# A transformer layer on one core: loads and waits of x's last tokens, of the attention's first pair, and of five modulation steps put elsewhere in the order

## The chip, the cores and the metric

The kernel runs on one core of a Trainium2 chip. The metric is the device time of one execution in microseconds (us), lower is better; several runs are made, and their median is compared. A core has five engines, each with its own instruction queue worked off in order: TensorE (PE in the profile; its weight loads are PEld), VectorE (DVE), ScalarE (ACT), GpSimd (POOL) and SyncE (SP, which here issues most of the DMAs). Engines wait for one another on semaphores.

## The reference, cut to what matters

One layer over 512 latent tokens x and 256 context tokens ctx, width 1024, in float32: a SwiGLU half-step, two mixers side by side (a neighbourhood attention and a gated delta rule) merged by gates, and a second SwiGLU half-step. Shift, scale and gate of each sublayer are columns of silu(c) @ w_ada.

```python
def ffn_sublayer(h, m, i, w_up, w_down):
    shift, scale, gate = sub_mod(m, i)
    y = swiglu(modulate(h, shift, scale), w_up, w_down)
    return post_ln(DEEPNORM_ALPHA * h + 0.5 * gate * y, ln_g[i], ln_b[i])
x = ffn_sublayer(x, mod_x, 0, ffn1_w_in, ffn1_w_out)
ctx = ffn_sublayer(ctx, mod_c, 0, ffn1_w_in, ffn1_w_out)
qa, ka, va, qkv_b, z_b, a_b, b_b, ga, gb = split_proj(modulate(x, shift_x, scale_x) @ w_in)
...
o_a = na_latent(grid(qa), grid(ka), grid(va), kc_h, vc_h, na_rpb)
o_b = gdn_output(o_lat2[0] + jnp.flip(o_lat2[1], axis=2), z_b, gdn_norm_w)   # o * norm * silu(z)
y = sigmoid(ga) * (o_a @ w_pa) + sigmoid(gb) * (o_b @ w_pb)
x = post_ln(DEEPNORM_ALPHA * x + gate_x * (y @ w_o), ln_g[1], ln_b[1])
x = ffn_sublayer(x, mod_x, 2, ffn2_w_in, ffn2_w_out)
```

## The kernel before

Matmuls are made in three passes: each float32 operand is split into a rounded high part (a cast on ACT) and the rest (a subtraction on DVE), and high x high, high x low and low x high are summed in PSUM. So nearly every tile exists as a pair: weights are loaded raw (wr, ra), cast to wh on ACT (`split`, L137) and subtracted to wl on DVE (L139); modulated tokens become uxh and uxl in the same way, and the mixer's output obh and obl.

A scheduler orders the instructions of each engine from their data and from its own timeline; `tc.issue_after(x)` holds the instructions inside it behind instruction x. Tiles come from pools with a fixed number of buffers, so a load waits until the tile's last reader is done. `Stream` loads and splits the weights some steps ahead; `behind` names, for an item, the instructions behind which its cast and its subtraction are put. `marks` holds instructions that such waits name.

Three places matter.

*The third section's steps.* The first half-step runs its units over x, then eight units over the context tokens (N1 = 8, f from 0; 48 matmuls each). Between units `ada_step` runs a step of `ada_gen`: it loads 128 rows of w_adaT (512 KB), and DVE multiplies them with silu(c) for x and for ctx and sums them up (two instructions of L280, tile adap). With the last row tile of a section one instruction (L303) adds the bias to colx, one to colc. Behind the units, TensorE transposes these columns to rows (`to_row`, L242), and the down projection follows (L211).

*The last tokens of x.* Behind the first half-step's down projection of x, `finish1` normalises each of the four blocks of 128 tokens (y), and `to_u` transposes y on TensorE, scales and shifts it on ACT into u (four pieces of 128 columns to a half, L151), and splits each half into uxh and uxl. These run beside the context's down projection. Its end frees PSUM tiles through `evac1` (DVE: h, L635, then x1c, L636), and then come the projections into the mixers: `fill_spill` multiplies uxh and uxl with w_in's columns for z, 24 matmuls to a group; in the order the first three groups are ps_5263, ps_5298 and ps_5333, with the weights wh_5174, wh_5180 and wh_5259. `finish1(fc, "c", ...)` normalises the context tokens (squares on ACT, L644; DVE, L649 and L651; y at L660), beside these.

*The attention's first pair.* `attend` works on a pair of heads m and four blocks b of 128 queries: scores on TensorE (sc, L1446), bias and maximum on DVE (L1448, L1450), exponentials on ACT (pr, L1454), transposes of pr on TensorE and their copies on ACT (pT, L1463), values transposed on TensorE (from vst) and copied by DVE (vw, L1430), and the product po (L1472). `att_load` loads qa, ka, kc, bias and va of the next pair and splits them. The lines ahead of the pairs load the delta rule's output ob and its gate z from DRAM, multiply them on DVE (L1491) and split the product; `gated` multiplies it with w_pb in slots between the blocks.

## Time and profile before

| | us |
|---|---|
| three runs | 1501.2, 1498.06, 1495.04 |
| median | 1498.06 |
| the profiled execution's own time | 1493.83 |
| its span (first to last instruction) | 1492.1 |
| TensorE busy | 1436.7 (96%) |
| VectorE busy | 1146.2 (77%) |
| ScalarE busy | 662.5 (44%) |
| GpSimd busy | 214.5 (14%) |
| 248.56 MB moved | mean 167 GB/s |

The mean granted clock of TensorE over the span was 0.99 of full speed. A row of a timeline gives the start, the length, engine, line, operation, output<-input with shapes, the count, and in brackets how long the engine had been idle ahead of it and what ended that.

### The profile page before, as it was taken

To read this page: it belongs to the slowest core of one execution; us is meant where nothing else is said; L and a number is where in the kernel's file an instruction comes from. 1 tells how busy PE (TensorE), PEld (TensorE's weight loads), DVE (VectorE), ACT (ScalarE), POOL (GpSimd) and SP (SyncE) were. 2 spreads that over 40 slices of the span, in tenths; PEclk is the share of its full clock that TensorE was granted. 3 is DMA by queue.
4 is the path that set the end of the run, shared out by engine and by line. 5 is a ranking of instruction groups with operands and counts; after the bars stand their busy time and mean duration, and the time that the engine had idled before them with its cause. 6 is when DMAs were issued, how large, how long until landed. Compare 5 with 4: busy or idle time off the path is not lost.

```text
span 1492.1 us, 23919 instructions
## 1 busy us (share of the span) xinstructions
PE 1436.7 (96%) x9117; PEld 1259.7 (84%) x9117; DVE 1146.2 (77%) x1975; ACT 662.5 (44%) x1090; POOL 214.5 (14%) x262
## 2 busy tenths in 40 slices
PE   6999999999999999999999899989999999999997
PEld 4789889999998777989887778867788999998886
DVE  8686969999987565768787896667668799886627
ACT  5435513434333286546544434367526454444310
POOL 1000000000000121323301002242321022220001
PEclk9999999999999999999999999999999999999999
DMA  9675764444569443222477523374244133233732
GB/s 371 208 257 212 254 239 174 151 171 156 170 210 401 178 174 121 93 92 81 152 231 205 171 68 125 105 254 140 99 170 156 57 132 109 88 111 136 261 98 84
DMA packets 109236, 248.56 MB, mean 167 GB/s; under 512 B 29049, under 2 KB 44481, under 8 KB 109121
## 3 DMA queue, kind: packets, MB, share of 16 engines
q1 hardware_dynamic: 104480, 229.40, 45.3%
q0 software_dynamic: 3056, 12.33, 2.2%
q10 hardware_dynamic: 1586, 5.32, 0.9%
q8 instruction: 71, 1.16, 0.3%
q14 instruction: 43, 0.35, 0.1%
HBM read 215.50 MB, written 31.50 MB: 166 GB/s over the span
## 4 chain that ended last, share of the span: by engine, by line
PE 72%; DVE 11%; DMA 9%; issue 3%; ACT 3%; POOL 2%; SPq 1%; DVEq 0%; ACTq 0%; POOLq 0%
PE ps L211 15%; PE pm L192 5%; PE pm L193 5%; PE pm L194 5%; PE ps L535 4%; PE ps L534 4%; PE ps L533 4%; PE ps L193 4%; PE ps L194 4%; PE ps L192 4%; PE ps L1692 3%; PE ps L1694 3%; PE ps L1693 3%; PE pc L1049 2%; DVE wl L139 2%
## 5 line engine op out<-in xcount | busy, mean ns | idle before, releaser
L139 DVE TENSOR_TENSOR wl<-wr,wh 128x1024 fp32r<-128x1024 f32 (+1 forms) x184 | 225.9, 1232 | 117.6 <-ACT wh L137 117.2
L137 ACT CAST wh<-wr 128x1024 fp32r<-128x1024 f32 (+1 forms) x184 | 185.3, 1013 | 265.1 <-PE pm L193 63.9
L192 PE MATMUL pm<-uxh,wh 128*128 128x512 f32 x320 | 131.7, 412 | 0.0
L194 PE MATMUL pm<-uxh,wl 128*128 128x512 f32 x320 | 126.5, 395 | 1.6 <-DVE wl L139 1.6
L193 PE MATMUL pm<-uxl,wh 128*128 128x512 f32 x320 | 126.2, 395 | 0.0
L211 PE MATMUL ps<-wh,hx 128*128 128x512 f32 x352 | 95.9, 391 | 0.7 <-ACT wh L137 0.7
L211 PEld LDWEIGHTS ps<-wh,hx 128*128 128x128 f32 x352 | 65.9, 188 | 15.1 <-ACT wh L137 1.1
L280 DVE SCALAR_TENSOR_TENSOR adap<-wr,crow 128x1024 f32<-128x1024 f32 x61 | 74.3, 1218 | 0.7 <-ACT crow L288 0.3
L194 PEld LDWEIGHTS pm<-uxh,wl 128*128 128x128 f32 x320 | 60.8, 190 | 14.8 <-DVE wl L139 1.8
L192 PEld LDWEIGHTS pm<-uxh,wh 128*128 128x128 f32 x320 | 60.9, 190 | 11.0 <-ACT spill L796 0.2
L193 PEld LDWEIGHTS pm<-uxl,wh 128*128 128x128 f32 x320 | 61.0, 191 | 10.4
L192 PE MATMUL ps<-uh,wh 128*128 128x256 f32 (+1 forms) x208 | 68.5, 329 | 0.8 <-ACT wh L137 0.8
L193 PE MATMUL ps<-ul,wh 128*128 128x256 f32 (+1 forms) x208 | 67.7, 325 | 0.0
L194 PE MATMUL ps<-uh,wl 128*128 128x256 f32 (+1 forms) x208 | 67.6, 326 | 0.0
L114 POOL TENSOR_TENSOR rs<-ve,mhalf 128x1 f32<-128x1 f32 (+2 forms) x46 | 47.3, 1030 | 139.8 <-DVE ve L110 137.4
L193 PE MATMUL ps<-uxl,wh 128*128 128x256 f32 (+1 forms) x192 | 61.3, 321 | 1.6 <-DVE uxl L139 1.6
L192 PE MATMUL ps<-uxh,wh 128*128 128x256 f32 (+1 forms) x192 | 60.6, 323 | 1.6 <-ACT uxh L137 1.4
L194 PE MATMUL ps<-uxh,wl 128*128 128x256 f32 (+1 forms) x192 | 60.9, 320 | 0.0
L137 ACT CAST wh<-ra 128x1024 fp32r<-128x1024 f32 x31 | 32.6, 1052 | 60.3 <-PE ps L534 20.2
L533 PE MATMUL ps<-ur,wh 128*128 128x384 f32 x168 | 56.5, 336 | 0.0
L534 PE MATMUL ps<-ur,wh 128*128 128x384 f32 x168 | 56.4, 336 | 0.0
L533 PE MATMUL ps<-uh,wh 128*128 128x384 f32 x168 | 56.4, 336 | 0.0
(502 smaller groups left out, 4257.6 us busy)
## 6 DMA issues: line engine op xcount, KB each, us to landing
wr<-in_w_adaT_dram SPq DMA_DIRECT2D x64, 512.0 KB, 4.7
wr<-in_up_dram SPq DMA_DIRECT2D x56, 512.0 KB, 3.5
wr<-in_win_dram SPq DMA_DIRECT2D x52, 512.0 KB, 3.3
wr<-in_dn_dram SPq DMA_DIRECT2D x51, 512.0 KB, 3.5
...
```

The costliest lines, as they stand in the source:

```text
L114: G.tensor_tensor(rs[:], ve[:], mhalf[:, 0:n], ALU.pow)
L137: S.copy(hi, src)
L139: marks["lo"] = V.tensor_tensor(lo, src, hi.bitcast(F32), ALU.subtract).ins
L192: T.matmul(ps, a, uh[:, k, :], start=(k == 0), stop=False)
L193: T.matmul(ps, a, ul[:, k, :], start=False, stop=False)
L194: marks["mm"] = T.matmul(ps, b, uh[:, k, :], start=False, stop=(k == nk - 1)).ins
L211: T.matmul(banks[t][d][:, c0:c1], a[:, sl], b[:, d * 512 + c0:d * 512 + c1], start=first and j == 0, stop=last and j == 2)
L280: V.scalar_tensor_tensor(pr[:], raw[:], 1.0, crow, op0=ALU.mult, op1=ALU.mult, accum_out=col[:, c:c + 1])
L533: T.matmul(ps[:], a, mh, start=k == 0, stop=False)
L534: T.matmul(ps[:], a, ml, start=False, stop=False)
L535: T.matmul(ps[:], b, mh, start=False, stop=k == 3)
L1692: T.matmul(ps[:], a, uh[:, k], start=k == 0, stop=False)
```

## The change

The third section's five extra steps stand in other context units; x's last token block is scaled and split half by half, with the work that stood beside it put behind; and the loads and products of ob and z go into the attention's first pair, in tiles of yb, with the next pair's casts put behind named copies.

```diff
@@ -134,11 +134,11 @@
     def split(src, hi, lo, behind=()):
 
         with tc.issue_after(behind[0]) if behind and behind[0] else nullcontext():
-            S.copy(hi, src)
+            marks["hi"] = S.copy(hi, src).ins
         with tc.issue_after(behind[1]) if behind else nullcontext():
             marks["lo"] = V.tensor_tensor(lo, src, hi.bitcast(F32), ALU.subtract).ins
 
-    def to_u(tp, pp, xn, uh, ul, c0, scale, shift, tag="u32", behind=()):
+    def to_u(tp, pp, xn, uh, ul, c0, scale, shift, tag="u32", behind=(), halves=False):
 
         u32 = tl(tp, [P, KT, P], tag)
         for hb in range(2):
@@ -146,9 +146,10 @@
             for q in range(4):
                 k = hb * 4 + q
                 T.transpose(ps[:, q, :], xn[:, k * P:(k + 1) * P], ident)
-            for q in range(4):
-                k = hb * 4 + q
-                S.activation(u32[:, k, :], ps[:, q, :], AF.Identity, bias=shift[:, k:k + 1], scale=scale[:, k:k + 1])
+            with tc.issue_after(marks["hi"]) if halves and hb else nullcontext():
+                for q in range(4):
+                    k = hb * 4 + q
+                    S.activation(u32[:, k, :], ps[:, q, :], AF.Identity, bias=shift[:, k:k + 1], scale=scale[:, k:k + 1])
             ks = slice(hb * 4, hb * 4 + 4)
             split(u32[:, ks], uh[:, ks, c0:c0 + P], ul[:, ks, c0:c0 + P], behind)
         return u32
@@ -476,7 +477,7 @@
     for f in range(N1):
         hc.append(h_c())
         ffn_unit(tp, pp, ws.get(), ws.get(), uch, ucl, NCT, *hc[-1])
-        ada_step(f in (2, 3, 4, 5, 6))
+        ada_step(f in (0, 1, 3, 4, 5))
     rows_out(tp, "fs", 2)
     accd = tl(dp, [6, P, D], "accd")
     sild = tl(dp, [1, D], "sild")
@@ -665,7 +666,9 @@
 
     def u2(p, pp, kind, t, y):
         uh, ul, col = (uxh, uxl, colx) if kind == "x" else (uch, ucl, colc)
-        to_u(p, pp, y, uh, ul, t * P, secs(col, 4), secs(col, 3))
+        to_u(p, pp, y, uh, ul, t * P, secs(col, 4), secs(col, 3), halves=kind == "x" and t == 3)
+        if kind == "x":
+            ux_done[:] = marks["hi"], marks["lo"]
 
     wp2, close_wp2 = pool("w1b")
     NT = 4
@@ -730,9 +733,10 @@
 
     def after(t, j, banks):
         if j == NT - 1:
-            nms.append(evac1(lp, banks, x1c[t], x1c[t], gc))
-
-    FIN1 = (0, 2, 5, 8)
+            with tc.issue_after(ux_done[1]) if t else nullcontext():
+                nms.append(evac1(lp, banks, x1c[t], x1c[t], gc))
+
+    FIN1, ux_done = (0, 2, 5, 8), []
     down(pp, ws, hc, 2, 0, tail[:-NT], between, after, post=tail[-NT:], n=N2)
     order = [("z", m) for m in range(4)]
     for h in range(4):
@@ -743,6 +747,7 @@
     order += [(n, m) for n in ("pb", "pa") for m in range(8)]
     src = [I["wab"] if n == "ab" else I["w" + n][m] if n in ("pa", "pb") else I["win"][WIN_IDX[(n, m)]] for n, m in order]
     ws2 = Stream(wp, [(w, "a") if j < 24 and j % 3 == 2 else w for j, w in enumerate(src)], WB, 2)
+    ws2.behind = {1: tuple(ux_done), 2: tuple(ux_done)}
     ws2.fill(2)
     close_wp2()
     close_lp()
@@ -1004,7 +1009,8 @@
         for _ in fill_spill(ga_, "z", m, zd):
             pass
         if m > 1:
-            ys.append(finish1(fc, "c", len(ys), x1c[len(ys)], nms[4 + len(ys)]))
+            with tc.issue_after(ux_done[0]), tc.issue_after(ux_done[1]):
+                ys.append(finish1(fc, "c", len(ys), x1c[len(ys)], nms[4 + len(ys)]))
     units = []
     for h in range(4):
         units += [decay()] * (h == 2) + [unit_q(h), unit_k(h), unit_v(h), unit_kc(h), unit_vc(h)]
@@ -1365,13 +1371,14 @@
     close_gb()
     ne, close_ne = pool("ne", "right")
 
-    def att_load(p, m):
+    def att_load(p, m, behind=(None, None)):
 
         qk = []
         for n, c, src in (("qa", NX, qad), ("ka", NX, kad), ("kc", NCT, kcd)):
             hi, lo = tl(p, [P, c], n + "h", 1, F32R), tl(p, [P, c], n, 1, F32R)
             nc.sync.dma_start(lo[:].bitcast(F32), src[m])
-            S.copy(hi[:], lo[:].bitcast(F32))
+            with tc.issue_after(behind[0]) if behind[0] else nullcontext():
+                S.copy(hi[:], lo[:].bitcast(F32))
             G.tensor_tensor(lo[:], lo[:].bitcast(F32), hi[:].bitcast(F32), ALU.subtract)
             qk.append((hi[:], lo[:]))
         bias = tl(p, [P, 3, 2, 256], "bias")
@@ -1380,8 +1387,9 @@
         nc.sync.dma_start(va[:], vad[m])
         w = tl(p, [P, 4, 8, 32], "vst")
         pv = va[:].rearrange("p (r c) -> p r c", c=64)
-        for b in range(4):
-            S.copy(w[:, b], pv[:, :, NA_C0[b]:NA_C0[b] + 32])
+        with tc.issue_after(behind[1]) if behind[1] else nullcontext():
+            for b in range(4):
+                S.copy(w[:, b], pv[:, :, NA_C0[b]:NA_C0[b] + 32])
         return *qk, bias, w
 
     ready = att_load(ne, 0)
@@ -1452,7 +1460,7 @@
             sm = tl(na_, [P, 2], "sm", 4)
             for i in range(2):
                 S.activation(pr[:, i], sc[:, i], AF.Exp, bias=nm[:, i:i + 1], accum_out=sm[:, i:i + 1])
-            V.reciprocal(sm[:], sm[:])
+            marks["rec"] = V.reciprocal(sm[:], sm[:]).ins
             for i in range(2):
                 G.tensor_scalar(dg[b // 2][:, b % 2, i], ident, sm[:, i:i + 1], None, op0=ALU.mult)
             for i in range(2):
@@ -1460,10 +1468,12 @@
                 for q in range(4):
                     T.transpose(pt[:, q, :], pr[:, i, q * P:(q + 1) * P], ident)
                 pT = tl(na_, [P, 4, P], "pT", 4)
-                S.copy(pT[:], pt[:])
+                marks["pT", b] = S.copy(pT[:], pt[:]).ins
                 pts.append(pT)
             if b == 0:
                 vw = att_values(w)
+            if m == 0:
+                ob_part(b)
 
             for q in range(4):
                 for i, pT in enumerate(pts):
@@ -1483,13 +1493,20 @@
             nc.sync.dma_start(dbg["oa"][:, m], oa[:])
         split(oa[:], oah[:, m], oal[:, m])
 
-    for m in range(4):
-        ob = tl(na_, [P, NX], "ob", 2)
-        nc.sync.dma_start(ob[:], obd[m])
-        z = tl(na_, [P, NX], "z", 2)
-        nc.sync.dma_start(z[:], zd[m])
-        V.scalar_tensor_tensor(ob[:], z[:], 0.5, ob[:], op0=ALU.mult, op1=ALU.mult)
-        split(ob[:], obh[:, m], obl[:, m])
+    def ob_load(m):
+        nc.sync.dma_start(yb[:, m], obd[m])
+        nc.sync.dma_start(yb[:, 4 + m], zd[m])
+
+    def ob_part(b):
+
+        for m in (2 * b - 4, 2 * b - 3):
+            if 0 <= m < 4:
+                split(yb[:, m], obh[:, m], obl[:, m], (marks["pT", 2], marks["rec"]))
+        for m in (2 * b - 2, 2 * b - 1):
+            if 0 <= m < 4:
+                with tc.issue_after(marks["rec"]):
+                    V.scalar_tensor_tensor(yb[:, m], yb[:, 4 + m], 0.5, yb[:, m], op0=ALU.mult, op1=ALU.mult)
+
     spool[0] = na_
 
     def gated(name, gd, m, oh, ol):
@@ -1506,6 +1523,9 @@
     def between(m, b, scores):
 
 
+        if m == 0 and b < 2:
+            ob_load(2 * b)
+            ob_load(2 * b + 1)
         if m == 3:
             wso.fill(b + 1)
         if (m, b) in SLOTS:
@@ -1528,7 +1548,7 @@
             for _ in fills:
                 pass
         if m < 3:
-            ready = att_load((na_, ne)[m % 2], m + 1)
+            ready = att_load((na_, ne)[m % 2], m + 1, (marks["pT", 1] if m == 0 else None, marks["pT", 2 - 2 * m] if m < 2 else None))
     close_na()
     close_pg()
     close_pm()
```

In the rows below, an engine's instructions stand in their order; x2 or x4 at a row's end counts like instructions in succession, and the numbers behind a name tell tiles apart.

*The third section.* DVE, from the last two adap products to the last instruction on colc, ahead of the down projection (wl_1578 is the first weight tile of that; colx and colc belong to x and ctx). Before:

```order
L139 TENSOR_TENSOR hc_1492<-fs_1555,hc_1492 128x256
L280 SCALAR_TENSOR_TENSOR adap_1562,colx_72<-wr_1560,crow_83 128x1024
L280 SCALAR_TENSOR_TENSOR adap_1564,colc_73<-wr_1560,crow_83 128x1024
L303 SCALAR_TENSOR_TENSOR colx_72<-colx_72,bcol_71 128x8
L139 TENSOR_TENSOR wl_1578<-ra_1575,wh_1577 128x1024
L139 TENSOR_TENSOR wl_1661<-wr_1658,wh_1660 128x1024
L303 SCALAR_TENSOR_TENSOR colc_73<-colc_73,bcol_71 128x8
```

Now:

```order
L139 TENSOR_TENSOR hc_1424<-fs_1487,hc_1424 128x256
L281 SCALAR_TENSOR_TENSOR adap_1494,colx_72<-wr_1492,crow_83 128x1024
L139 TENSOR_TENSOR wl_1572<-ra_1569,wh_1571 128x1024
L274 TENSOR_TENSOR fs_1563<-fs_1563,ps_1514 128x256
L281 SCALAR_TENSOR_TENSOR adap_1496,colc_73<-wr_1492,crow_83 128x1024
L304 SCALAR_TENSOR_TENSOR colx_72<-colx_72,bcol_71 128x8
L139 TENSOR_TENSOR wl_1578<-ra_1575,wh_1577 128x1024
L139 TENSOR_TENSOR hc_1500<-fs_1563,hc_1500 128x256
L304 SCALAR_TENSOR_TENSOR colc_73<-colc_73,bcol_71 128x8
```

The last two products now stand apart, two to three rows earlier, the one row tile's load being a unit earlier; colc's bias stands behind wl_1578 and hc_1500 and ahead of wl_1661.

*The last tokens of x.* ACT, from the casts of the third block (u_905) on; u_929 is the fourth block, wh_5180 and wh_5259 the second and third of z's weights. Before:

```order
L137 CAST wh_5180<-wr_5178 128x1024
L137 CAST uxh_4690<-u_905_4970 128x4x128 x2
L151 ACTIVATE u_929_5071<-ps_5072,colx_72 128x128 x4
L151 ACTIVATE u_929_5071<-ps_5083,colx_72 128x128 x4
L644 ACTIVATE sq_5362,ss_5363<-x1c_842_4742,nm_5131 128x1024
L137 CAST uxh_4690<-u_929_5071 128x4x128
L137 CAST wh_5259<-wr_5257 128x1024
L137 CAST uxh_4690<-u_929_5071 128x4x128
L644 ACTIVATE sq_5374,ss_5375<-x1c_842_4742,nm_5372 128x1024
```

Now:

```order
L661 ACTIVATE y_928_5068<-ax_722_4078,nb_5066,rs_926_5064 128x1024
L137 CAST uxh_4690<-u_905_4970 128x4x128 x2
L152 ACTIVATE u_929_5071<-ps_5072,colx_72 128x128 x4
L137 CAST uxh_4690<-u_929_5071 128x4x128
L152 ACTIVATE u_929_5071<-ps_5083,colx_72 128x128 x4
L137 CAST uxh_4690<-u_929_5071 128x4x128
L137 CAST wh_5180<-wr_5178 128x1024
L137 CAST wh_5259<-wr_5257 128x1024
L645 ACTIVATE sq_5362,ss_5363<-x1c_842_4742,nm_5131 128x1024
L137 CAST wh_5294<-wr_5292 128x1024
```

The cast of the first half of u_929 now stands between the two halves of u, and both weight casts and the squares of the context tokens stand behind its second half. On TensorE the first matmuls on u_929's halves; before:

```order
L192 MATMUL ps_5263<-uxh_4690,wh_5174 128x512
L192 MATMUL ps_5298<-uxh_4690,wh_5180 128x512
L192 MATMUL ps_5333<-uxh_4690,wh_5259 128x512
L193 MATMUL ps_5263<-uxl_4691,wh_5174 128x512
L194 MATMUL ps_5263<-uxh_4690,wl_5175 128x512
L192 MATMUL ps_5263<-uxh_4690,wh_5174 128x512
```

Now:

```order
L193 MATMUL ps_5263<-uxh_4690,wh_5174 128x512
L194 MATMUL ps_5263<-uxl_4691,wh_5174 128x512
L195 MATMUL ps_5263<-uxh_4690,wl_5175 128x512
L193 MATMUL ps_5263<-uxh_4690,wh_5174 128x512
L194 MATMUL ps_5263<-uxl_4691,wh_5174 128x512
```

Before, the first matmul of three groups stood in front; now the first group stands whole.

*The attention's first pair.* ACT, from the first pr on: pT_9631 and pT_9638 are the first block's copies (9607 and 9614 now). Before:

```order
L1454 ACTIVATE pr_9619,sm_9620<-sc_9603,nm_9617 128x512 x2
L1454 ACTIVATE pr_9677,sm_9678<-sc_9661,nm_9675 128x512 x2
L137 CAST obh_9564<-ob_9570 128x512
L137 CAST obh_9564<-ob_9577 128x512
L1374 CAST qah_9879<-qa_9880 128x512
L137 CAST wh_9923<-wr_9921 128x512
L796 COPY spill_9876<-pm_9851 128x512
L1463 COPY pT_9631<-pt_9626 128x512
L1374 CAST kah_9884<-ka_9885 128x512
L1463 COPY pT_9638<-pt_9633 128x512
L1374 CAST kch_9889<-kc_9890 128x256
```

Now:

```order
L1462 ACTIVATE pr_9595,sm_9596<-sc_9575,nm_9593 128x512 x2
L1462 ACTIVATE pr_9657,sm_9658<-sc_9637,nm_9655 128x512 x2
L1471 COPY pT_9607<-pt_9602 128x512
L1471 COPY pT_9614<-pt_9609 128x512
L1462 ACTIVATE pr_9704,sm_9705<-sc_9688,nm_9702 128x512 x2
L137 CAST wh_9915<-wr_9913 128x512
L801 COPY spill_9868<-pm_9843 128x512
L1471 COPY pT_9669<-pt_9664 128x512
L1471 COPY pT_9676<-pt_9671 128x512
L1381 CAST qah_9871<-qa_9872 128x512
L1381 CAST kah_9876<-ka_9877 128x512
L1381 CAST kch_9881<-kc_9882 128x256
```

The two pT stand right behind the four pr, and the casts of ob's product (obh) and of qa, ka and kc behind the next block's. On DVE, before:

```order
L1491 SCALAR_TENSOR_TENSOR ob_9570<-z_9572,ob_9570 128x512
L1455 RECIPROCAL sm_9620<-sm_9620 128x2
L1491 SCALAR_TENSOR_TENSOR ob_9577<-z_9579,ob_9577 128x512
L1455 RECIPROCAL sm_9678<-sm_9678 128x2
L139 TENSOR_TENSOR obl_9565<-ob_9570,obh_9564 128x512
L139 TENSOR_TENSOR obl_9565<-ob_9577,obh_9564 128x512
L139 TENSOR_TENSOR wl_9924<-wr_9921,wh_9923 128x512
L1448 TENSOR_TENSOR sc_9706<-sc_9706,bias_8666 128x2x256
L1450 TENSOR_REDUCE nm_9720<-sc_9706 128x2
L1448 TENSOR_TENSOR sc_9751<-sc_9751,bias_8666 128x2x256
L1430 COPY vw_9640<-pt_9641 128x512
L1430 COPY vw_9640<-pt_9647 128x512
```

Now:

```order
L1463 RECIPROCAL sm_9596<-sm_9596 128x2
L1463 RECIPROCAL sm_9658<-sm_9658 128x2
L1508 SCALAR_TENSOR_TENSOR yb_9566<-yb_9566 128x512 x2
L1456 TENSOR_TENSOR sc_9688<-sc_9688,bias_8666 128x2x256
L1458 TENSOR_REDUCE nm_9702<-sc_9688 128x2
L1438 COPY vw_9616<-pt_9617 128x512
L1438 COPY vw_9616<-pt_9623 128x512
L1456 TENSOR_TENSOR sc_9739<-sc_9739,bias_8666 128x2x256
L1463 RECIPROCAL sm_9705<-sm_9705 128x2
L1508 SCALAR_TENSOR_TENSOR yb_9566<-yb_9566 128x512 x2
L1458 TENSOR_REDUCE nm_9753<-sc_9739 128x2
```

The first two products of z and ob stand behind the two reciprocals and ahead of the third block's bias and of vw; the other two stand ahead of the fourth block's maximum; the obl are behind all of these. On SP, the eight loads of ob and z now stand together, behind vc's and ahead of kad's write and of the loads of qa, ka and kc; before, four stood there, and the other four after ka, among the later loads.

## The prediction, made before the changed kernel was run

> **What bounds the kernel now.** I read the page's first part, then the chain that ended last, then TensorE's own timeline for its waits, and last the windows around those that the change touches.

> ```profile
> span 1492.1 us, 23919 instructions
> PE 1436.7 (96%) x9117; PEld 1259.7 (84%) x9117; DVE 1146.2 (77%) x1975; ACT 662.5 (44%) x1090; POOL 214.5 (14%) x262
> PE 72%; DVE 11%; DMA 9%; issue 3%; ACT 3%; POOL 2%; SPq 1%; DVEq 0%; ACTq 0%; POOLq 0%
> ```

> TensorE is busy for 96% of the span, so 1492.1 - 1436.7 = 55.4 us of its idle time, in some thirty short gaps, is all that an edit of the order can win directly. The change adds and removes hardly any arithmetic. So I price it by the gaps that it touches: which end, which stay, and what is late next. What comes after each place is busy TensorE again, and I take it that a gap closed there brings the end nearer by its length.

> **The third section's steps.** In each row: start, length, engine, line, operation, output<-input, and in brackets the idle time ahead of it with what ended it.

> ```profile
> 162.62 1.23 DVE L280 SCALAR_TENSOR_TENSOR adap<-wr,crow 128x1024 f32<-128x1024 f32 x1
> 163.42 1.05 ACT L137 CAST wh<-ra 128x1024 fp32r<-128x1024 f32 x1 [0.68 <-DMA ra<-in_dn_dram]
> 165.65 1.22 DVE L139 TENSOR_TENSOR wl<-wr,wh 128x1024 fp32r<-128x1024 f32 x1
> 166.78 0.16 DVE L303 SCALAR_TENSOR_TENSOR colc<-colc,bcol 128x8 f32<-128x8 f32 x1
> 167.00 0.27 PE L242 MATMUL ps<-ident,colc 128*8 128x128 f32 x1 [1.80 <-DVE colc L303]
> 145.98 1.99 ACT L137 CAST wh<-wr 128x1024 fp32r<-128x1024 f32 x2 [1.63 <-DMA wr<-in_up_dram]
> 147.08 0.39 PE L192 MATMUL ps<-uh,wh 128*128 128x256 f32 x1 [0.39 <-ACT wh L137]
> ```

> Five steps stay five: each is one 512 KB load of w_adaT on SP and two column products of 1.23 us on DVE, moved and not added. The last pair now runs one unit earlier, so colc is no longer the last thing that DVE does before TensorE transposes it. The load of ra in the second row also moves up on SP, past the last w_adaT load that stood ahead of it. In the new order colc's last instruction stands behind wl of that ra, behind which the following matmuls wait anyway. I take all 1.80 us as won. The cover is DVE's spare time in the units before; if it is gone, what is late next is a weight load: ACT at 145.98 waits 1.63 us for one, and TensorE lost 0.39 us at 147.08 on it. With w_adaT in units 0, 1, 3, 4 and 5 the same ring of buffers is asked for as much, earlier, so waits of that kind can end, stay, or come twice. Bounds of this part: 1.80 - 1.63 = 0.2 us (one such wait shows in full) and 1.80 + 0.39 = 2.2 us. I take 1.8, nearest to the row.

> **The last tokens of x.**

> ```profile
> 557.01 2.90 ACT L151 ACTIVATE u<-ps,colx 128x128 f32<-128x128 f32 x8 [3.26 <-DVE x1c L636]
> 559.76 1.18 ACT L644 ACTIVATE sq<-x1c,nm 128x1024 f32<-128x1024 f32 x1
> 560.90 0.64 ACT L137 CAST uxh<-u 128x512 fp32r<-128x512 f32 x1
> 561.40 1.08 ACT L137 CAST wh<-wr 128x1024 fp32r<-128x1024 f32 x1
> 562.35 0.66 ACT L137 CAST uxh<-u 128x512 fp32r<-128x512 f32 x1
> 561.82 1.28 DVE L649 SCALAR_TENSOR_TENSOR x1c<-x1c,nm,lng 128x1024 f32<-128x1024 f32 x1
> 563.63 0.68 DVE L139 TENSOR_TENSOR uxl<-u,uxh 128x512 fp32r<-128x512 f32 x1
> 561.59 0.74 PE L192 MATMUL ps<-uxh,wh 128*128 128x512 f32 x2 [1.39 <-ACT uxh L137]
> 562.54 0.50 PE L192 MATMUL ps<-uxh,wh 128*128 128x512 f32 x1 [0.21 <-ACT wh L137]
> 564.37 0.50 PE L193 MATMUL ps<-uxl,wh 128*128 128x512 f32 x1 [1.33 <-DVE uxl L139]
> 582.23 0.49 PE L148 MATMUL ps<-ident,y 128*128 128x128 f32 x3
> ```

> Now ACT does eight pieces of u, then squares for a layer norm that nobody waits for, then uxh; DVE does layer norm before uxl. TensorE waits 1.39 + 0.21 + 1.33 = 2.93 us. After the change ACT's row is four u, uxh, four u, uxh, and the two weight casts and the squares come behind. From 557.01: four pieces take half of 2.90, so the first uxh begins at 558.5 and ends at 559.1; uxl follows by 559.8. Four more u end near 560.6, the second uxh near 561.2, its uxl near 561.9. TensorE ends the work before at 561.59 - 1.39 = 560.2. Its first group, all 24 matmuls of ps_5263, needs wh_5174, which stands ahead of all this on ACT; the first 12 need the first half alone. At 0.22 us each (14 in 3.06 us, the window of 568.94 below), the second half is wanted at 562.8 and the next weights, wh_5180, at 560.2 + 5.3 = 565.5. Two casts of 1.08 us behind 561.2 end at 563.4, and DVE's wl two rows behind. So none of the three waits stays: 2.93 us.

> What is queued behind the new waits: layer norm of context tokens (x1c, squares) begins behind two weight casts, near 563.4 where it began at 559.76, 3.6 us later, and TensorE asks for its y first at 582.23. I cost that at nothing; the cover, those 19 us for squares, two passes of DVE and y, is gone if it slips by some 10 more.

> Behind the gaps comes a second loss, in the granted clock. A window's columns: length, busy time of PE, PEld, DVE, ACT and POOL with counts, granted clock, DMA share, GB/s.

> ```profile
> 562.11:565.52 3.41, 1.88 (x7) 1.17 (x7) 3.41 (x6) 0.90 (x2) 0.19 (x1) 1.00 0.00 0
> 565.52:568.94 3.42, 3.42 (x10) 2.65 (x9) 1.92 (x5) 1.37 (x3) 0.08 (x1) 0.50 0.67 229
> 568.94:572.00 3.06, 3.06 (x14) 2.51 (x14) 1.45 (x2) 2.25 (x3) 2.44 (x5) 1.00 0.48 146
> 165.20:168.60 3.40, 1.60 (x8) 1.34 (x9) 3.40 (x6) 2.15 (x5) 0.00 (x0) 1.00 0.78 284
> ```

> A window of 3.41 us in which TensorE had been idle for 1.53 is followed by 3.42 us at 0.50, full of matmuls: half of it, 1.7 us, is lost. A full row of matmuls in the first window would keep the clock at 1.00, as in nearly every slice of the page. Sum of this part 2.93 + 1.7 = 4.6; bounds 2.9 (the half clock stays) and 4.6.

> [...]

> **The attention's first pair.**

> ```profile
> 971.68 0.69 DVE L1491 SCALAR_TENSOR_TENSOR ob<-z,ob 128x512 f32<-128x512 f32 x1 [2.49 <-DMA z<-zd]
> 972.95 0.69 DVE L1491 SCALAR_TENSOR_TENSOR ob<-z,ob 128x512 f32<-128x512 f32 x1 [0.51 <-DMA z<-zd]
> 972.40 0.62 ACT L137 CAST obh<-ob 128x512 fp32r<-128x512 f32 x1 [1.67 <-DVE ob L1491]
> 976.05 0.59 ACT L1463 COPY pT<-pt 128x512 f32<-128x512 f32 x1
> 976.96 0.68 DVE L1448 TENSOR_TENSOR sc<-sc,bias 128x512 f32<-128x512 f32 x1
> 977.68 1.22 DVE L1450 TENSOR_REDUCE nm<-sc 128x2 f32<-128x1024 f32 x1
> 979.41 1.28 DVE L1430 COPY vw<-pt 128x512 f32<-128x512 f32 x2
> 976.69 0.66 PE L1429 MATMUL pt<-ident,vst 128*128 128x128 f32 x4 [2.38 <-ACT pT L1463]
> 977.69 0.65 PE L1429 MATMUL pt<-ident,vst 128*128 128x128 f32 x4 [0.35 <-ACT pT L1463]
> 980.15 1.12 PE L1472 MATMUL po<-pT,vw 128*64 128x128 f32 x8 [1.80 <-DVE vw L1430]
> 983.40 2.78 POOL L1457 TENSOR_SCALAR z<-ident,sm 128x128 f32<-128x128 f32 x4 [4.22 <-PE pt L1461]
> 971.72:975.13 3.41, 2.58 (x33) 2.21 (x31) 2.77 (x6) 1.84 (x4) 0.00 (x0) 1.00 1.04 395
> 975.13:978.54 3.41, 1.31 (x8) 0.84 (x8) 2.81 (x3) 2.82 (x7) 2.57 (x3) 1.00 1.02 359
> 978.54:981.95 3.41, 1.80 (x16) 1.58 (x16) 3.35 (x6) 2.71 (x9) 0.64 (x1) 0.50 1.02 377
> 981.95:985.36 3.41, 3.41 (x19) 2.57 (x17) 1.38 (x2) 2.88 (x7) 1.96 (x3) 0.50 0.98 330
> ```

> Here pT, transposed before TensorE stops at 976.69 - 2.38 = 974.3, waits on ACT behind two obh, qah, wh and a spill, and vw waits on DVE behind the same tiles. Idle: 2.38 + 0.35 + 1.80 = 4.53 us. Half clock: of the two windows at 0.50 TensorE worked 1.80 + 3.41 = 5.2 us, so 2.6 are lost. In all 7.1 us can be won.

> After the change pT goes straight behind the four pr. But on DVE both products of ob and z, still waiting for their loads, now stand ahead of the third score tile and vw. The second load ends at 972.95; vc's 128 KB goes ahead of it now, 0.35 us at the windows' 380 GB/s. So: the products end at 974.0, the scores' bias (0.68) at 974.7, their maximum (1.22) at 975.9, the first half of vw near 976.6, and with it po begins, 3.5 us before 980.15. TensorE keeps four fill matmuls (0.9 us) for just that place and has work until about 975 (974.3 and vst's transposes, which no longer wait), so 1.6 us of idle time stay. Another wait of about 1 us is likely near 982, for the fourth token block's pr, since DVE puts the other two products ahead of its maximum. With both of these and one of the two half-clock windows (1.7) left, the gain is 7.1 - 1.6 - 1.0 - 1.7 = 2.8; with the first wait alone 5.5. I take 3.0, near the lower of these, since an idle time of 1.5 us in one window was enough for the half clock above.

> On SP all eight loads of ob and z (256 KB each) now go ahead of kad, qa, ka, kc; four of them went behind. At 380 GB/s 1 MB is 2.7 us: qa, ka and kc of the second pair land that much later. On POOL ka's low half then stands behind six z (0.7 us each, 2.78 for four) and qa's; I estimate it near 982.6, and TensorE wants it near 982. DMA share is 1.0 here, so bounds of this part run from -2 (the 2.7 us show in full and only 0.7 of the idle time goes) to 5.5.

> **Sum.** 1.8 + 4.6 + 3.0 = 9.4, against this execution's own time of 1493.83 us (span 1492.1, 1.7 outside it): 1484.4. The three runs' median, 1498.06, lies 4.2 above it, so by the median 1498.06 - 9.4 = 1488.7; I say 1489. Runs of this kernel spread by 3 us to either side. Faster by over 0.5% (7.5 us, about what a measurement can tell here) begins at 1490.6.

> **Rivals.**
> - The attention's gain is eaten by its own loads. For it: a DMA share of 1.0 and DVE's products standing in order ahead of vw. Against: only two of the four products do, and the loads they need go out as early as before. Gain there -2 to 1, sum 6.4 - 0.5 = 5.9, time 1492.
> - The half clock does not go with the gaps. For it: 1.60 busy of 3.40 at 165.20 left the clock at 1.00 and 1.88 of 3.41 did not, so busy time alone does not decide it. The x part gives 2.9, the attention 1.3: 1.8 + 2.9 + 1.3 = 6.0, time 1492.
> - Slower: the loads of the third section. If every one of the five steps makes a weight load late by the 1.63 us of the row at 145.98, and nothing covers it, TensorE loses 8.2 us where it lost 0.4, and colc's 1.80 is not won either, its unit's load being late as well. With the other parts at their lower bounds (2.9 and -2) the sum is -7.8 + 2.9 - 2.0 = -6.9 and the time 1505. With those bounds it ends slower than before from 0.3 us a step on. Against: of ACT's 1.63 us only 0.39 reached TensorE.
> - No change that shows: the gaps close and the time comes back at the next place where TensorE waits for DVE or a load, since the scheduler moved rows elsewhere too. Time 1498.

> **Chances.** Forecast (a sum of 5 to 12.3, 1485.8 to 1493) 0.60, of it 0.47 past 1490.6; attention eaten 0.13; half clock stays 0.10; no change 0.08, of it 0.03 past the bound on the faster side by the spread; the loads of the third section 0.09, of it 0.07 past the bound. So faster 0.47 + 0.03 = 0.50, slower 0.07, same 0.43. The range, 1483 to 1499, takes in the upper bounds with the spread of the runs, and reaches to the case without change; it leaves out the slower case and little else.

> **What would show it.** In the profile after: TensorE's transpose of colc without a wait; no gap over 0.3 us where ps_5263 begins, and clock 1.00 for the 10 us behind; pT right behind the fourth pr; one gap of 1.5 to 2.5 us ahead of the first po, ended by DVE's vw; and ka's low half on POOL not being what ends a wait of TensorE. The forecast is wrong if weight loads end waits in the third section, if vw ends a gap over 3.5 us, or if a gap that was small before has grown elsewhere.

## The result, and the profile after

The changed kernel took 1483.13 us in the median of six runs (1480.26 to 1486.92), the kernel before 1498.55 in six (1495.04 to 1501.2, the three from above among them): 15.4 us less by the two medians. The ratio of the runs on record is 0.9909 with a 95% interval of 0.9892 to 0.9927, which makes 13.6 us, between 10.9 and 16.2. It is not the ratio of the two medians (0.9897); what follows goes by it, unless it says otherwise. A second set of six runs, the last row but one of the table below, gave 0.9894 (0.9876 to 0.9911). The kernel is faster by clearly more than the 7.5 us that a measurement can tell here. The profiled execution took 1482.26 us, against 1493.83 before.

The page of the changed kernel, the lines that were shown of before:

```profile
span 1480.5 us, 23912 instructions
PE 1430.8 (97%) x9117; PEld 1255.9 (85%) x9117; DVE 1144.0 (77%) x1975; ACT 661.7 (45%) x1090; POOL 214.6 (14%) x262
```

TensorE does the same 9117 matmuls. Its idle time fell by 5.7 us (1480.5 - 1430.8 = 49.7, from 55.4) and its busy time by 5.9 us. In the stretches at a granted clock of 0.50 TensorE was busy for 21.5 us before and for 9.9 us in the change, half of the difference being 5.8 us, and matmuls of 256 columns come closer (0.1133 us from start to start against 0.1178, last section). So the page says that half of the gain between the two profiles isn't idle time.

Of the third section, the timeline of the changed kernel:

```profile
161.81 0.15 DVE L304 SCALAR_TENSOR_TENSOR colc<-colc,bcol 128x8 f32<-128x8 f32 x1
162.73 0.27 PE L243 MATMUL ps<-ident,colc 128*8 128x128 f32 x1
151.36 0.38 PE L193 MATMUL ps<-uh,wh 128*128 128x256 f32 x1 [0.44 <-ACT wh L137]
```

The transpose of colc has no bracket: colc is ready at 161.96, 0.8 us before TensorE comes to it. One wait for a late weight is left (0.44 us), where there were two: 0.39 at 147.08 and this one of before:

```profile
148.02 0.38 PE L192 MATMUL ps<-uh,wh 128*128 128x256 f32 x1 [0.44 <-ACT wh L137]
```

Of x's last tokens, the same view:

```profile
552.58 1.50 ACT L152 ACTIVATE u<-ps,colx 128x128 f32<-128x128 f32 x4 [4.21 <-PE ps L148]
554.12 0.62 ACT L137 CAST uxh<-u 128x512 fp32r<-128x512 f32 x1
554.64 1.50 ACT L152 ACTIVATE u<-ps,colx 128x128 f32<-128x128 f32 x4
556.18 0.62 ACT L137 CAST uxh<-u 128x512 fp32r<-128x512 f32 x1
556.70 2.00 ACT L137 CAST wh<-wr 128x1024 fp32r<-128x1024 f32 x2
558.61 1.15 ACT L645 ACTIVATE sq<-x1c,nm 128x1024 f32<-128x1024 f32 x1
556.83 0.69 DVE L139 TENSOR_TENSOR uxl<-u,uxh 128x512 fp32r<-128x512 f32 x1 [1.37 <-ACT uxh L137]
555.61 0.39 PE L193 MATMUL ps<-uxh,wh 128*128 128x512 f32 x1
591.32 0.39 PE L193 MATMUL pm<-uch,wh 128*128 128x256 f32 x1 [0.62 <-ACT uch L137]
592.21 0.39 PE L194 MATMUL pm<-ucl,wh 128*128 128x256 f32 x1 [0.50 <-DVE ucl L139]
595.58 0.66 PE L927 MATMUL pg<-ident,convc 128*128 128x128 f32 x4 [0.40 <-ACT convc L921]
```

ACT does four u, uxh, four u, uxh, and only then the weight casts and the squares; the first matmul of ps_5263, at 555.61, doesn't wait. In the last three rows stands the price: the context tokens' uch and ucl are now late, and so is convc behind them. Three waits of 0.62, 0.50 and 0.40 us have come, 1.52 in all, where TensorE was busy before.

Of the attention's first pair:

```profile
965.57 1.08 ACT L1471 COPY pT<-pt 128x512 f32<-128x512 f32 x2 [0.67 <-PE pt L1469]
966.62 0.69 DVE L1508 SCALAR_TENSOR_TENSOR yb<-yb 128x512 f32<-128x512 f32 x1 [0.76 <-DMA yb<-zd]
967.96 1.22 DVE L1458 TENSOR_REDUCE nm<-sc 128x2 f32<-128x1024 f32 x1
969.10 1.28 DVE L1438 COPY vw<-pt 128x512 f32<-128x512 f32 x2
967.44 1.09 PE L1437 MATMUL pt<-ident,vst 128*128 128x128 f32 x8
968.77 0.50 PE L195 MATMUL pm<-uxh,wl 128*128 128x512 f32 x1
969.57 0.40 PE L195 MATMUL pm<-uxh,wl 128*128 128x512 f32 x1
969.90 0.66 PE L1482 MATMUL po<-pT,vw 128*64 128x128 f32 x8
972.28 0.43 PE L1482 MATMUL po<-pT,vw 128*64 128x128 f32 x2 [0.26 <-ACT pT L1471]
975.07 1.26 POOL L1382 TENSOR_TENSOR ka<-ka,kah 128x512 fp32r<-128x512 f32 x1
```

DVE's second product does wait for its load (0.76 us), and vw does stand behind it, the scores' bias and their maximum. But the first half of vw is ready near 969.8, and TensorE is at work until 969.90: behind the transposes of vst it has four fill matmuls (pm, 968.77 to 969.57; projections that need nothing of this stage), and po follows them at once. There is no gap ahead of the first po, and 0.26 us later on.

The windows around both places, before and then the changed kernel (length, busy time of PE, PEld, DVE, ACT, POOL, granted clock, DMA share, GB/s):

```profile
555.00:575.00 20.00, 17.07 (x70) 13.10 (x69) 13.14 (x27) 10.94 (x21) 3.99 (x16) 0.91 0.30 99
960.00:980.00 20.00, 14.45 (x106) 11.41 (x104) 13.14 (x19) 10.90 (x24) 5.94 (x7) 0.96 0.74 259
```

```profile
555.00:575.00 20.00, 20.00 (x90) 16.54 (x89) 15.86 (x25) 13.62 (x20) 4.68 (x15) 1.00 0.39 123
960.00:980.00 20.00, 19.70 (x163) 15.00 (x161) 14.79 (x24) 14.53 (x36) 11.56 (x11) 1.00 1.00 369
```

The granted clock is 1.00 in both after, and 0.91 and 0.96 before.

### The profile page after: what moved, and what is told of

Its sections match the earlier page's. It is cut to its first block, busy times and chain, and to the rows that moved or that the text cites. A ratio compares the mean times of both kernels' runs of the same rounds, so it can differ in the third digit from the quotient of the medians.

```text
span 1480.5 us, 23912 instructions
## 1 busy us (share of the span) xinstructions
PE 1430.8 (97%) x9117; PEld 1255.9 (85%) x9117; DVE 1144.0 (77%) x1975; ACT 661.7 (45%) x1090; POOL 214.6 (14%) x262
## 4 chain that ended last, share of the span: by engine, by line
PE 72%; DVE 11%; DMA 8%; issue 3%; ACT 3%; POOL 2%; SPq 1%; DVEq 0%; POOLq 0%; ACTq 0%
PE ps L212 17%; PE ps L534 5%; PE ps L536 5%; PE ps L535 5%; PE pm L193 4%; PE pm L194 4%; PE pm L195 4%; PE ps L193 3%; PE ps L195 3%; PE ps L194 3%; PE ps L1712 3%; PE ps L1714 3%; PE ps L1713 3%; PE pc L1055 2%; DVE wl L139 2%
## 5 line engine op out<-in xcount | busy, mean ns | idle before, releaser
L137 ACT CAST wh<-wr 128x1024 fp32r<-128x1024 f32 (+1 forms) x184 | 185.4, 1013 | 270.6 <-PE pm L194 67.5
L139 DVE TENSOR_TENSOR wl<-wr,wh 128x1024 fp32r<-128x1024 f32 (+1 forms) x184 | 225.1, 1228 | 102.2 <-ACT wh L137 101.8
L193 PE MATMUL pm<-uxh,wh 128*128 128x512 f32 x320 | 131.3, 410 | 0.2
L114 POOL TENSOR_TENSOR rs<-ve,mhalf 128x1 f32<-128x1 f32 (+2 forms) x46 | 50.3, 1095 | 141.5 <-DVE ve L110 139.1
L193 PEld LDWEIGHTS pm<-uxh,wh 128*128 128x128 f32 x320 | 60.7, 190 | 11.3 <-ACT u L152 0.4
L194 PEld LDWEIGHTS pm<-uxl,wh 128*128 128x128 f32 x320 | 60.7, 190 | 10.4
L193 PE MATMUL ps<-uh,wh 128*128 128x256 f32 (+1 forms) x208 | 68.2, 328 | 0.4 <-ACT wh L137 0.4
L137 ACT CAST wh<-ra 128x1024 fp32r<-128x1024 f32 x31 | 32.6, 1052 | 62.1 <-PE ps L535 20.2
L193 PE MATMUL ps<-uxh,wh 128*128 128x256 f32 (+1 forms) x192 | 59.7, 317 | 0.0
```

What stands on the lines that cost most here:

```text
L114: G.tensor_tensor(rs[:], ve[:], mhalf[:, 0:n], ALU.pow)
L137: marks["hi"] = S.copy(hi, src).ins
L139: marks["lo"] = V.tensor_tensor(lo, src, hi.bitcast(F32), ALU.subtract).ins
L193: T.matmul(ps, a, uh[:, k, :], start=(k == 0), stop=False)
L194: T.matmul(ps, a, ul[:, k, :], start=False, stop=False)
```

## The experiments

All but two were timed against the kernel before on the same chip. Beside the ratio and the time saved by it, the table shows a local reading of the profiles: how much earlier the same matmuls start than in the profile of before (median over 8 us), and by how much that lead grew across three stretches of before's time: 120 to 180 us (third section), 526 to 625 (x's tokens up to the context's projections), 960 to 1010 (first pair). Each is one execution, and one of these stretches that a kernel's edits don't touch shows -2.3 to 1.2 us. The longer stretch from 740 to 960 us, in which no kernel has an edit, lost 0.9 to 6.6 us in all thirteen profiles against this one of before, so the three leads don't add up to the gain.

| kernel | ratio (95%) | us saved | third | x | att. | fills behind vst |
|---|---|---|---|---|---|---|
| the change | 0.9909 (0.9892, 0.9927) | 13.6 | 3.6 | 4.5 | 6.0 | 4 |
| e1: third section alone | 0.9977 (0.9963, 0.9992) | 3.4 | 3.4 | 1.3 | 1.2 | - |
| e2: x alone | 0.9972 (0.9960, 0.9984) | 4.2 | -1.0 | 3.2 | 0.2 | - |
| e3: attention alone | 0.9981 (0.9967, 0.9994) | 2.8 | -0.3 | -0.8 | 4.6 | 0 |
| e10: without third section | 0.9930 (0.9906, 0.9954) | 10.5 | 0.5 | 3.8 | 3.3 | 0 |
| e11: without x | 0.9943 (0.9922, 0.9965) | 8.5 | 2.8 | 1.3 | 5.8 | 3 |
| e4: change, context norm free | 0.9919 (0.9899, 0.9939) | 12.1 | 3.4 | 5.0 | 3.1 | 0 |
| e5: e3, six fills held back | 0.9979 (0.9964, 0.9995) | 3.1 | -2.3 | -0.8 | 4.3 | 6 |
| e6: e4, six fills held back | 0.9924 (0.9900, 0.9949) | 11.4 | 3.4 | 5.0 | 4.9 | 6 |
| e9: the change again | 0.9894 (0.9876, 0.9911) | 15.9 | 4.2 | 4.8 | 6.1 | 4 |
| e12: change less halves, six held | 0.9898 (0.9879, 0.9918) | 15.3 | 3.4 | 5.5 | 4.1 | 6 |

**One part at a time.** e1 changes one line of before:

```diff
-        ada_step(f in (2, 3, 4, 5, 6))
+        ada_step(f in (0, 1, 3, 4, 5))
```

> Only the third section's steps are put in units 0, 1, 3, 4 and 5; all else as before. Theory (the parts add up, each worth its closed gaps and half-clock windows): 3 us faster than before, that is the 1.80 us gap at colc's transpose, 0.4 us of waits for late weight loads, and about 1 us spread over the eight units. Rival (the forecast's term): 1.8 us, colc's gap alone. Rival (the parts lean on one another): within 1 us of before, because the gain stands only with the others. In the profile: no wait at the transpose of colc.

It saved 3.4 us, where 1.8 was forecast; the interval, 1.2 to 5.5, holds that, and the 3 that was expected of it here. Its profile shows neither colc's gap nor the two waits at 147.08 and 148.02, and one thing more, some 380 us behind the edit. Before had a gap that the prediction does not name:

```profile
543.86 1.09 PE L148 MATMUL ps<-ident,y 128*128 128x128 f32 x8 [1.15 <-ACT y L660]
```

e1 has no wait there: the scheduler put the transposes of this y behind 100 of the down projection's 168 matmuls, where they stood behind 108, and y itself comes earlier. All seven profiles with the third section's line have that order and no wait, all seven without it the old order and a wait. In e2, which leaves the third section as it was, the gap is there (1.55 us):

```profile
542.89 1.09 PE L148 MATMUL ps<-ident,y 128*128 128x128 f32 x8 [1.55 <-ACT y L661]
594.53 0.39 PE L193 MATMUL pm<-uch,wh 128*128 128x256 f32 x1 [0.65 <-ACT uch L137]
```

Against it, two waits at 515 and 517 grew to 0.90 and 0.85 us in e1, from 0.46 and 0.39.

e2 makes only the edits of x's tokens:

```diff
+            with tc.issue_after(marks["hi"]) if halves and hb else nullcontext():
...
+            with tc.issue_after(ux_done[1]) if t else nullcontext():
...
+    ws2.behind = {1: tuple(ux_done), 2: tuple(ux_done)}
...
+            with tc.issue_after(ux_done[0]), tc.issue_after(ux_done[1]):
```

> Only the last tokens of x: halves, and the context's eviction, the two weight casts and the context's layer norm behind them. Theory (parts add up): 4 us faster, that is 2.9 of gaps, 1.7 of half clock and 1.15 of the earlier gap ahead of y's transposes at 543, less about 1.5 us of new waits for the context tokens' u near 590. Rival (the forecast's term): 4.6 us with nothing lost behind. Rival (the gap at 543 closed by the third section's lead, not by this part): 1.15 less, 3 us, and the gap at 543 stands in the profile.

The three waits and the half clock of that place are gone (granted clock 1.00 from 550 to 580 us), the waits near 594 have come (row above, and 0.48 us for convc), and 4.2 us are saved, 2.4 to 6.0. So the gap at 543 belongs to the third section's edit, and the wait for uch near 590 to this one. The wait for convc comes with either: it is 0.34 us in e1, which doesn't touch x's tokens.

e3 makes only the attention's edits (`att_load`, `attend`, `ob_load`, `ob_part`, `between`).

> Only the attention's first pair: loads and products of ob and z in tiles of yb and the next pair's casts behind named copies. Theory (parts add up): 6 us faster, all 4.5 us of the gaps at 974 to 980 and the 2.6 us of half clock, less some tenths. Rival (the forecast's term): 3.0 us, with an idle time of 1.6 us ahead of the first po and one half-clock window left. Rival (the clock windows fall elsewhere, so a half-clock window comes by chance of their phase): 4.3 us, with gaps closed and one window at 0.50 between 970 and 990.

Its timeline, and two windows of 3.41 us on the grid that the last section tells of:

```profile
976.49 0.68 DVE L139 TENSOR_TENSOR wl<-wr,wh 128x512 fp32r<-128x512 f32 x1
978.95 0.69 DVE L1450 TENSOR_TENSOR sc<-sc,bias 128x512 f32<-128x512 f32 x1
979.55 1.28 DVE L1432 COPY vw<-pt 128x512 f32<-128x512 f32 x2
980.29 0.66 PE L1476 MATMUL po<-pT,vw 128*64 128x128 f32 x8 [1.73 <-DVE vw L1432]
```

```profile
978.38:981.79 3.41, 1.68 (x22) 1.33 (x21) 3.41 (x5) 1.45 (x4) 0.00 (x0) 1.00 1.06 405
981.79:985.20 3.41, 3.17 (x30) 2.25 (x28) 1.60 (x5) 3.20 (x8) 2.55 (x3) 1.00 1.06 404
```

Here a gap of the forecast's size stands, 1.73 us ahead of the first po, ended by vw (1.6 were forecast). But it comes from orders that the forecast didn't have: on DVE a wl and the fourth block's bias stand ahead of vw, and all 24 fill matmuls went ahead of vst's transposes. The change as a whole has those two instructions behind vw, and 20 fills ahead and four behind. No half clock follows here (granted clock 1.00 in both windows), though TensorE was idle for 1.73 of the first one's 3.41 us.

**What the attention's order depends on.** e4 takes one wait out of the change, the one that holds the context's layer norm:

```diff
-            with tc.issue_after(ux_done[0]), tc.issue_after(ux_done[1]):
-                ys.append(finish1(fc, "c", len(ys), x1c[len(ys)], nms[4 + len(ys)]))
+            ys.append(finish1(fc, "c", len(ys), x1c[len(ys)], nms[4 + len(ys)]))
```

> The changed kernel, but the layer norm of the context tokens (finish1 with c) isn't held behind the last uxh and uxl. Theory (that hold makes the context tokens late, and TensorE waits 1.5 us for them near 590 to 595): 1 to 1.5 us faster than the changed kernel, 14.5 to 15 us faster than before, with those waits gone and none of the first z group's coming back. Rival (the squares then stand between the halves of u again and delay the second half): as fast or up to 1 us slower than the changed kernel, with a gap of about 0.5 to 1 us at the first z group's second half. Rival (the context's wait near 590 has another cause, ACT's own row of u): no difference, the waits stay.

```profile
553.93 1.15 ACT L645 ACTIVATE sq<-x1c,nm 128x1024 f32<-128x1024 f32 x1
557.15 0.50 PE L194 MATMUL ps<-uxl,wh 128*128 128x512 f32 x1 [0.92 <-DVE uxl L139]
974.77 0.92 PE L1481 MATMUL po<-pT,vw 128*64 128x128 f32 x8 [1.93 <-DVE vw L1437]
```

The squares slip in ahead of the first uxh (555.06), and a wait of 0.92 us comes in place of the waits for uch near 590 (0.34 us for convc is left). And 400 us further on the attention has a gap of 1.93 us that the change doesn't have: all fills again went ahead. The two times, 12.1 and 13.6 us, can't be told apart. To see whether the fills' place decides the attention, e5 and e6 hold the last six of them behind vst's transposes:

```diff
+                marks["vT"] = T.transpose(ps[:, q, :], wf[:, b, kt * P:(kt + 1) * P], ident).ins
...
-            for _ in fills:
-                pass
+            while done[0] < len(FILLS) * FS - 1:
+                next(fills)
+            with tc.issue_after(marks["vT"]):
+                for _ in fills:
+                    pass
```

> The attention's first pair alone, as in the run of that part alone, and one order more: the last two steps (six matmuls, 1.4 us) of the last fill group are held behind the transposes of vst, where the changed kernel has four of them. Theory (the 1.73 us of idle time ahead of the first po in that run stood because the scheduler had put all 24 fill matmuls in front, so the part alone lacks the filler that the changed kernel has): the gap ahead of po falls under 0.5 us, no half-clock window between 970 and 990, and 1.5 to 3 us faster than the part alone, 4.5 to 6 us faster than before. Rival (vw is late by itself, behind the loads): the gap stays over 1 us, since the fill only moves the wait, and the time is that of the part alone, 2.8 us faster than before.

> The changed kernel without the hold on the context tokens' layer norm, with the same last fill steps held behind the transposes of vst. Theory (the run without the hold lost in the attention, where the scheduler then put all fill matmuls in front, what it won near 590): 1.9 us of gap and a half-clock window at 975 go, 14 to 16 us faster than before, as fast as the changed kernel or up to 1.5 us faster. Rival (the gap of 0.9 us that came at the first z group, and not the attention, is what made it slower): the attention's gap goes and the time stays at 12 us faster than before, the loss standing elsewhere.

Of e5's timeline:

```profile
979.98 0.66 PE L1476 MATMUL po<-pT,vw 128*64 128x128 f32 x8 [0.34 <-DVE vw L1432]
986.53 0.39 PE L1448 MATMUL sc<-ka,qah 64*128 64x256 f32 x2 [0.54 <-POOL ka L1376]
```

The gap falls from 1.73 to 0.34 us, but part comes back as a new wait for ka on POOL, the late load that the prediction had feared. In e5's time nothing is to be seen (0.9979 against e3's 0.9981), and in e6's neither (0.9924 against e4's 0.9919), though the lead grows by 4.9 in place of 3.1 us at that place. A difference of 1 to 2 us is below what these runs can tell, so the fills' place is shown in the traces alone.

And these traces show that the fills are only part of it. Counted from the transposes of oacc with which the stage begins (957.93 in the change, 966.93 in e3), TensorE has done its work ahead of the first po after 12.0 us where fills stand behind, and after 11.6 where all stand ahead (e3, e4, e10). The first half of vw is done after 11.8 to 12.4 us in the first kind, and after 13.3 to 13.5 in the second: only there do the wl and the fourth block's bias stand ahead of it, which take 1.2 us of DVE. So of e3's gap about 1.4 us are vw's and 0.4 TensorE's. The two orders came together in every profile, and no run set one without the other.

e10 and e11 take one part out of the change, the third section's line and the edits of x.

> The changed kernel with the third section's steps as before (units 2 to 6); the last tokens of x and the attention as in the change. Theory (parts add up, the attention with its whole fill group in front): 7 us faster than before, the sum of the two parts run alone (4.2 and 2.8). Rival (the parts lean on one another through the scheduler, and the third section brings the order that the attention needs): 4 to 5 us faster, or less.

> The changed kernel with the last tokens of x as before; the third section's steps and the attention as in the change (three fill matmuls behind vst's transposes here by the scheduler's own choice). Theory (parts add up): 3.4 + 3 = 6.4 us faster than before. Rival (with fill matmuls behind vst's transposes the attention gives 5 to 6): 8.5 to 9.5 us faster; the gap ahead of the first po is under 0.7 us.

Of e10's timeline, and a window:

```profile
164.49 0.27 PE L243 MATMUL ps<-ident,colc 128*8 128x128 f32 x1 [1.92 <-DVE colc L304]
975.51 0.87 PE L1482 MATMUL po<-pT,vw 128*64 128x128 f32 x8 [1.79 <-DVE vw L1438]
```

```profile
972.30:975.72 3.42, 1.63 (x20) 1.26 (x18) 3.39 (x6) 1.35 (x4) 0.00 (x0) 1.00 1.05 400
```

e10 differs from the change in one line, 800 us ahead of the attention, and yet its attention has the fills ahead, the wl and the bias ahead of vw, the gap of 1.79 us, and a clock of 0.51 in the window that follows. e11 put three fills behind and has no such gap. The line alone doesn't bring that order: e4 has it, and its fills stand ahead. Counted by what is missed when it is left out, the third section's line is worth 15.9 - 10.5 = 5.4 us, the x part 15.9 - 8.5 = 7.4 (the change, e10 and e11 ran on one chip); alone they brought 3.4 and 4.2. Part of that surplus is the attention's 6.0 against 3.3. But each of these differences is uncertain by 3 us or more, so that the parts bring more together than alone (13.6 or 15.9 against 3.4 + 4.2 + 2.8 = 10.4) is likely and not settled. The kernel without the attention's edits alone, e1 and e2 together, was not run.

**What in the x part does it.** e7 makes the halves and none of the new waits, e8 the waits and not the halves; each was profiled in one execution.

```diff
-        to_u(p, pp, y, uh, ul, t * P, secs(col, 4), secs(col, 3))
+        to_u(p, pp, y, uh, ul, t * P, secs(col, 4), secs(col, 3), halves=kind == "x" and t == 3)
```

> Of the last tokens of x only the halves: the second half of u stands behind the cast of the first uxh; weight casts, eviction and layer norm as before. Theory (TensorE waited for work that stood ahead of the splits, the squares, a weight cast and layer norm, more than for the second half of u): the first wait, 1.39 us, falls to under 0.9 us, the wait for uxl on DVE stays near 1 us, 1.5 to 2.2 us of gaps remain of 2.93. Rival (the halves alone do it): under 0.5 us of gaps remain.

> Of the last tokens of x all but the halves: eight u in a row, then both casts, with the two weight casts, the eviction and the context's layer norm behind. Theory: the first wait becomes about 0.5 us (the first cast ends 1.3 us earlier than now, near 560.6 of the clock of before, against TensorE's 560.2), the second and third go; 0.4 to 1.2 us of gaps remain of 2.93, no half-clock window behind. Rival (the halves are needed): 1.4 us or more remain.

Their single times, 1502.84 and 1493.86 us, say little. Of e7, then of e8, the waits and a window:

```profile
563.58 0.49 PE L193 MATMUL ps<-uxh,wh 128*128 128x512 f32 x1 [1.61 <-ACT wh L137]
550.00:580.00 30.00, 28.29 (x119) 22.25 (x118) 17.57 (x34) 19.81 (x35) 4.37 (x17) 0.94 0.25 86
```

```profile
560.42 0.50 PE L193 MATMUL ps<-uxh,wh 128*128 128x512 f32 x1 [0.28 <-ACT uxh L137]
561.14 0.50 PE L194 MATMUL ps<-uxl,wh 128*128 128x512 f32 x1 [0.23 <-DVE uxl L139]
550.00:580.00 30.00, 29.49 (x132) 23.76 (x131) 20.22 (x35) 19.94 (x33) 6.08 (x17) 1.00 0.40 132
```

With halves alone one wait of 1.61 us is left and the clock still drops (0.94 over 30 us). With the waits alone 0.28 + 0.23 us are left and the clock stays at 1.00. So it is the order of other work on ACT and DVE, the squares, the layer norm and the weight casts put behind, that wins the place; the halves add 0.5 us of gap closed.

The late uch near 590 needs both, and something else with them. TensorE waits for it in the four kernels that have the halves and the hold on the context's layer norm (the change, e9, e2, e10), and in none that lacks one of the two (e4, e6 and e7 the hold, e8 and e12 the halves). In those four, ACT also stands idle ahead of the squares of the second context block, for aex, a small tile. Its load stands on SP behind four of the weight loads; in e8 and e12 it stands behind three and nothing waits for it: counted from the first matmul of ps_5263 it is issued after 11.0 us there, and after 15.4 in the change. The change's row, then e12's (the next experiment):

```profile
576.47 0.21 ACT L883 ACTIVATE aex<-aex 128x8 f32<-128x8 f32 x1 [2.19 <-DMA aex<-in_a_log_dram]
571.61 0.21 ACT L883 ACTIVATE aex<-aex 128x8 f32<-128x8 f32 x1
```

e4 and e6 wait for aex too (2.59 and 3.29 us) and not for uch, so that load alone isn't enough either. Why the scheduler puts it there with the halves was not tried.

**The change again, and a simpler one.** e9 is the change unaltered, run to see whether what only its profile showed comes back; e12 drops the halves and holds six fills behind.

> The changed kernel itself once more, beside the others of this set. Theory (the spacing of the 256-column matmuls, 0.113 or 0.118 us, and the place of the half-clock windows change from run to run of the same order): 12 to 15 us faster than before again; in the profile the same gaps as in its first one within 0.5 us each, but in the third section the spacing can be 0.118 where it was 0.113. Rival (the spacing belongs to this program): 0.113 again between 122 and 145 us.

> A version that might be better: the changed kernel without the halves of x's last u (eight u, then both casts), and with the last six fill matmuls held behind vst's transposes. Theory (the halves aren't needed, and the hold fixes the attention's order whatever stands ahead): as fast as the changed kernel within 1.5 us, 12 to 15 us faster than before, no gap over 0.3 us at the first z group and none over 0.5 us ahead of the first po. Rival (the halves are worth their first 1.3 us): 1 to 2 us slower than the changed kernel, with a gap of that size at the first z group.

e9's profile has the same gaps as the first: no wait ahead of po, 0.61, 0.50 and 0.50 us near 590. e12 has neither the waits for uch near 590 (0.35 us for convc is left) nor the gap at 543, and in the attention 0.39 us ahead of the first po and 0.54 for ka, as e5 has them. At 0.9898 beside 0.9894 it is as fast as the change, and does not beat it.

## Why the prediction was right, and which of its steps were off

The forecast was faster, 1489 us in a range of 1483 to 1499; the median is 1483.13, inside the range by 0.13 us, which is luck. Against the profiled execution the sum was 9.4 us, and 1493.83 - 1482.26 = 11.6 were found. The mechanism held: three places, gaps closed, a half clock that goes with them. The sizes were off, and not all in one direction: the leads of the three places add up to 14.1 us, and 2.5 were lost elsewhere. That the sum came near is in part because these errors offset each other.

- **The third section's steps: 1.8 forecast; 2.8 to 4.2 found there in seven profiles, and 1.3 more at 543.** colc's 1.80 came as reckoned and no load took it back: of waits for late weights (0.39 + 0.44) one of 0.44 is left in the change and none in e1. By these gaps it is 2.2 and 2.6 us; the term took the waits for even, and the upper bound of 2.2 held one of the two alone. In the change closer matmul spacing (0.1133 us against 0.1178) adds at least 1 us (last section). What the step missed altogether is that the edit moves the scheduler's timeline, and with it y's transposes at 543: 1.15 us, less the 0.9 by which two waits near 517 grew.
- **The x part: 4.6 forecast, 3.2 found in e2** (4.5 in the change, with the third section's 1.3). The gaps (2.93) and the half clock (1.7) went as reckoned, by the order that the prediction worked out on ACT: it put the end of the second uxh 4.2 us behind u's start (561.2 less 557.01), and the trace has it there (556.18 + 0.62 - 552.58). What failed is the step that cost the later context layer norm at nothing. Its 19 us of cover held for y's transposes, but not for what comes behind them: uch and ucl are late, and 1.1 us come back near 590 in the change, 0.65 in e2. ACT's wait for aex, 2.19 and 1.90 us there, is in no term of the sum and used up part of the cover. The 0.4 us for convc aren't this part's, since e1 and e11 have them.
- **The attention: 3.0 forecast, 6.0 found.** Three losses were set against 7.1 us: 1.6 us of idle time ahead of po, 1.0 near 982 and 1.7 of half clock. In the change none is there but 0.26 us, and the clock is 1.00 from 960 to 1000 us. The first is the difference of two times, and both were off. Counted from oacc's transposes (963.75 before, 957.93 in the change), the forecast had TensorE out of work after 11.25 us (at 975) and the first half of vw done after 12.85 (at 976.6); the trace has 11.97 and 11.86. TensorE worked 0.7 us longer: 974.3 and vst's transposes (1.09) are 975.4 already, and the order with four fills behind has 0.3 more. vw came 1.0 us earlier, mostly since DVE began the second product after 8.69 us, where the load was expected after 9.55 (972.95 + 0.35); why it landed earlier is open. In e3, e4 and e10 the gaps of 1.73, 1.93 and 1.79 us look like the forecast's, but there vw is done after 13.3 to 13.5 us, behind two instructions that the prediction didn't count: that agreement is chance. The second was 0.24 + 0.23 + 0.29 us of small waits in e3, whose 4.6 us is about 7.1 less 1.73 less these. The half clock came behind the gap in e4 and e10 (granted clock 0.94 in both from 965 to 995 us) and not in e3 (1.00): a sure 1.7 should have been a chance. So even the upper bound, 5.5, which kept 1.6 us of idle time, was passed.
- **ka's low half on POOL** was not what ended a wait of TensorE in the change, but nearly: it was done at 976.33, and its first reader begins at 976.38. Counted as above, that is 982.1 on before's clock, where 982.6 was estimated. In e5, e6 and e12, with six fills held back, it does end a wait of 0.53 or 0.54 us.
- **The rivals.** The attention's gain was not eaten: alone it saved 2.8 us (0.9 to 4.9). The half clock did go with the gaps of x (0.91 to 1.00 in the windows); e7, with a gap of 1.61 us left, kept it (0.94 from 550 to 580 us). The loads of the third section took nothing. That the time comes back elsewhere happened in part: 1.5 us near 590, 0.9 near 517.
- **Its own signs.** Of the signs that it named for itself one did not come, the gap ahead of the first po. Of those that would make it wrong, two came in small: in the third section ACT waits 2.76 us for a weight load and TensorE 0.44 behind it, and the two waits near 517 grew from 0.85 to 1.74 us in the change.
- **The sum against the median.** The profiled execution of before was 4.7 us below its median of six (4.2 below that of three), of the change 0.9 below. So 11.6 us between the two profiles are 15.4 between the two medians, and 13.6 by the ratio. By any of the three the sum of 9.4 was too small.
